# Row maxima of an attention turned into a row by fp32r products with a rounded identity

## The chip, the cores and the metric

The kernel runs on one core of a Trainium2 chip. The time is the device time of one execution of the program in microseconds. Three executions of the kernel before took 2443.36, 2448.75 and 2449.61 us; their median is 2448.75 us. The profile was taken from a further execution of its own, of 2449.5 us.

## What is computed

Two layers of a hybrid backbone work on 1024 latent tokens and 256 context tokens of width 1024. Each layer projects its input once, and the columns of the projection feed three groups of heads: a bidirectional RWKV-7 scan (6 heads), a grouped-query attention (6 query heads over 2 key heads) and a neighbourhood attention (4 heads). The part that matters here is the softmax of the two attentions:

```python
def one_block(qi):
    s = jnp.einsum('bqgrd,bsgd->bgrqs', qi, keys).astype(jnp.float32)
    p = jax.nn.softmax(s, axis=-1).astype(vals.dtype)
    return jnp.einsum('bgrqs,bsgd->bqgrd', p, vals)
...
s = jnp.concatenate([s_nb.reshape(B, H, GRID_W, n_nb), s_ctx], axis=-1)
p = jax.nn.softmax(s, axis=-1).astype(v.dtype)
```

Here `s_nb` holds the scores inside a query's grid window with a learned bias, and `s_ctx` its scores against all context keys. A softmax may subtract any number from all scores of a query before the exponential, as long as it is one number for the query; the kernel subtracts a rough row maximum.

## The kernel before

**Stages.** Each of the two layers runs an input projection (L203 to L205), then the scan of the RWKV heads, `rwkv` (L516 to L828), and beside it `attention` (L831 to L1133), then the output projection (L1196 to L1198). The program is written as one function after the other, but a scheduler orders each engine's instructions from a simulation of its own, so that the scan and the attention end up woven together on every engine. Each engine then takes its instructions strictly in that order, the DMA issues on SP included.

**The scan** is a chain of 40 steps in each layer: products with the state that wait for a DMA load of `X` (L706, L713), a copy (L716), products (L724), copies (L730), products (L734) and a decay on VectorE (L739). Between steps stand waves of preparation: a 16x16 inverse on VectorE (L653, L655) that goes out to DRAM through `inv_d` (L666) and comes back as `di` (L670).

**The attention** works on pairs of jobs. A job is 512 queries of one head (128 of the context), a pair is two such jobs, and there are 30 pairs in both layers together. `pair_max` finds the row maxima of one pair while `pair_main` does the exponentials and the products with the values of the pair before. In `pair_max`, for each tile of 128 queries:

- L894: rough scores `sm` = queries by keys, in up to three pieces of at most 512 keys, into PSUM;
- L896 or L898: VectorE reduces each piece to its maximum `mx`;
- L901: VectorE reduces the maxima of the pieces to one negated column of `nm`, a tile of 128 x 8 fp32 values, one column for each tile of queries;
- L907: once all columns stand, a TensorE product turns a column into a row: `nm`'s column is the stationary operand (128 x 1), the identity the moving one (128 x 128), and the row goes to partition 64 of `mt`;
- L908: ScalarE copies the row, rounded to fp32r, to partition 64 of the query tile `q[1]`.

`pair_main` then makes the scores `st` by two products, L963 with 128 rows and L964 with 65 rows, of which the last is this row of negated maxima against a row of ones in the keys. So L964 waits for L908, and L908 for L907. The exponential is L970 or L973, the sums are L977 or L982, the products with the values L948.

**Types.** The operands of L894, L963, L964 and of both projections are fp32r; those of L907, L948 and the scan are fp32. The profile has two records of TensorE for each fp32 product and one for each fp32r product. So the 180 products of L907 (two layers) are 360 records.

Of the kernel before, what the change touches and what calls it, by code (L numbers as in the profile page):

```python
# [8 lines left out]
F32 = mybir.dt.float32  # L9
F32R = mybir.dt.float32r  # L10
AF = mybir.ActivationFunctionType
ALU = mybir.AluOpType
AX = mybir.AxisListType
# [30 lines left out]
def body(tc, a):  # L44
    nc = tc.nc
# [4 lines left out]
    def cload(name, shape, eng):  # L50
        t = const.tile(shape, F32, tag="c_" + name, name="c_" + name)
        eng.dma_start(out=t, in_=a[name])
        return t

    silu = cload("c_col", [128, KT, 2], nc.sync)
    ident = cload("ident", [128, 128], nc.gpsimd)
# [25 lines left out]
    def mod_load(pool, l, g, k):  # L82
        wt = pool.tile([128, 1024], F32, tag="wm", name="wm")
        nc.sync.dma_start(out=wt, in_=a["wmod"][l, k, :, 1024 * g:1024 * g + 1024])
        return wt

    def mod_out(pt, l, g):
        mo = mods[l][:, 8 * g:8 * g + 8, :]
        nc.vector.tensor_tensor(out=mo, in0=pt, in1=bmod[:, l, 8 * g:8 * g + 8].unsqueeze(2).to_broadcast([128, 8, 2]), op=ALU.add)
        if g == 1:  # L90
            nc.vector.tensor_scalar(out=mo, in0=mo, scalar1=1.0, scalar2=None, op0=ALU.add)

    def mod_spread(groups, pool, psum):

        todo = [(l, g, k) for l, g in groups for k in range(KT)]
        acc = pool.tile([128, 256], F32, tag="am", name="am")
        silu32 = pool.tile([128, KT, 32], F32, tag="silu32", name="silu32")
        nc.gpsimd.memset(silu32, 0.0)
        nc.gpsimd.tensor_copy(silu32[:, :, 0:2], silu)
        nxt = mod_load(pool, *todo[0])  # L100
        yield
        for i, (l, g, k) in enumerate(todo):
            pm = psum.tile([128, 512], F32, tag="st", name="pmod")
            for j in range(4):
                nc.tensor.matmul(out=pm[32 * j:32 * j + 32, 0:256], lhsT=silu32[:, k, :], rhs=nxt[:, 256 * j:256 * j + 256],
                                 start=True, stop=True, tile_position=(0, 32 * j))
            if k == 0:
                nc.vector.tensor_copy(acc, pm[:, 0:256])
            else:
                nc.vector.tensor_tensor(out=acc, in0=acc, in1=pm[:, 0:256], op=ALU.add)  # L110
            if i + 1 < len(todo):
                nxt = mod_load(pool, *todo[i + 1])
            yield
            if k == KT - 1:
                pt = psum.tile([128, 512], F32, tag="st", name="pt")[:, 0:16].rearrange("p (m j) -> p m j", j=2)
                for m in range(8):
                    q, c = 32 * (m // 2), 128 * (m % 2)
                    nc.tensor.matmul(out=pt[:, m, :], lhsT=acc[:, c:c + 128], rhs=ident[:, q:q + 2], start=True, stop=True)
                mod_out(pt, l, g)
                yield  # L120
# [710 lines left out]
    def attention(l):  # L831
# [4 lines left out]
        ap1 = es.enter_context(tc.tile_pool(name=f"at{l}", bufs=1, **kw))  # L836
        ap2 = es.enter_context(tc.tile_pool(name=f"au{l}", bufs=2, **kw))
        pst = es.enter_context(tc.tile_pool(name=f"pst{l}", bufs=2, space=PSUM, side="right"))
        py = es.enter_context(tc.tile_pool(name=f"py{l}", bufs=1, space=PSUM, side="right"))
        wn = es.enter_context(tc.tile_pool(name=f"wn{l}", bufs=1, **kw))  # L840
        ms = mod_spread(((1, 2),) if last else ((0, 2), (1, 1), (1, 0)), wn, pst)
        onec = ap1.tile([128, 32], F32, tag="onec", name="onec")
        nc.vector.memset(onec, 1.0)

# [37 lines left out]

        def pair_max(q, k, jobs, nq, bias):

            nm = ap2.tile([128, 8], F32, tag="nm", name="nm")
            for i, job in enumerate(jobs):
                q0 = job["q0"]
                for qt in range(nq // 128):
                    qc = q0 + 128 * qt
                    pcs = job["parts"](qt)  # L890
                    mx = ap2.tile([128, 4], F32, tag="mx", name="mx", bufs=4)
                    for n_, (c0, o, bcol) in enumerate(pcs):
                        sp_ = pst.tile([128, 512], F32, tag="sm", name="sm", bufs=2)
                        nc.tensor.matmul(out=sp_[:, :o], lhsT=q[0][:, qc:qc + 128], rhs=k[0][:, c0:c0 + o], start=True, stop=True)  # L894
                        if bcol is None:
                            nc.vector.tensor_reduce(out=mx[:, n_:n_ + 1], in_=sp_[:, :o], op=ALU.max, axis=AX.X)  # L896
                        else:
                            nc.vector.tensor_tensor_reduce(out=sp_[:, :o], in0=sp_[:, :o], in1=bias[0][:, bcol:bcol + o], scale=1.0, scalar=-3.0e38,  # L898
                                                           op0=ALU.add, op1=ALU.max, accum_out=mx[:, n_:n_ + 1])
                        if n_ == len(pcs) - 1:  # L900
                            nc.vector.tensor_reduce(out=nm[:, 4 * i + qt:4 * i + qt + 1], in_=mx[:, :len(pcs)], op=ALU.max, axis=AX.X, negate=True)  # L901
                        yield
            for i, job in enumerate(jobs):
                q0 = job["q0"]
                mt = pst.tile([128, 512], F32, tag="sm", name="mt", bufs=2)
                for qt in range(nq // 128):
                    nc.tensor.matmul(out=mt[64:65, 128 * qt:128 * qt + 128], lhsT=nm[:, 4 * i + qt:4 * i + qt + 1], rhs=ident, start=True, stop=True, tile_position=(0, 64))  # L907
                nc.scalar.copy(q[1][64:65, q0:q0 + nq], mt[64:65, :nq])  # L908
                yield

# [189 lines left out]
        while True:  # L1100
            nxt = next(hs, None)
            mg = None
            npc = 0
            if nxt is not None:
                q, k, v, jobs, nq, och, bias = nxt
                mg = pair_max(q, k, jobs, nq, bias)
                npc = sum(len(j["parts"](t)) for j in jobs for t in range(nq // 128)) + 2
            if cur is not None:
                q, k, v, jobs, nq, och, bias = cur
                nit = len(jobs[0]["steps"]) + 1  # L1110
                done = 0
                old, tail[:] = tail[:], []
                for i, _ in enumerate(pair_main(*cur, nxt is None)):
                    for f in old[:1 if i + 2 < nit else None]:
                        f()
                        old.pop(0)
                    n_it += 1
                    if n_it >= 20 and n_it % 3 == 0:
                        next(ms, None)
                    while mg is not None and done < npc * (i + 1) // nit:  # L1120
                        next(mg, None)
                        done += 1
            if mg is not None:
                for _ in mg:
                    pass
            cur = nxt
            if cur is None:
                break
# [202 lines left out]
    for l in range(DEPTH):  # L1331
        lay = {}
        layer_proj(l, hd, fw, lay, lambda: rwkv(l, lay))
        attention(l)
        so = ExitStack()
        with ExitStack() as es:
            ow = out_weights(l, so, es)
        hd = None if l == DEPTH - 1 else open_h(l + 1)
        fw = out_proj(l, so, ow, a["xT"] if l == 0 else x2_d, x2_d if l == 0 else a["out"], hd)
# [89 lines left out]
```

## Time and profile before

| | us |
|---|---|
| median of three executions | 2448.75 |
| the profiled execution | 2449.5 |
| its span, from the first to the last instruction | 2447.7 |
| TensorE busy | 2206.0 (90%) |
| VectorE busy | 1615.7 (66%) |
| products of L907, 360 records, busy | 52.8 |
| attention of layer 0: first rough scores, last product with values | 570.7, 1194.3 |
| attention of layer 1: the same | 1803.5, 2316.8 |

A busy TensorE is not one at its peak: matmuls overlap at their ends, so the busy times of records overlap too, and the pace of a product is read from the starts of two that follow each other. Windows of the trace give the busy time of each engine in a stretch, and the granted clock of TensorE there as a share of full speed.

### The profile page before, as it was taken

To read this page: it belongs to the slowest core of one execution; us is meant where nothing else is said; L and a number is where in the kernel's file an instruction comes from. 1 tells how busy PE (TensorE), PEld (TensorE's weight loads), DVE (VectorE), ACT (ScalarE), POOL (GpSimd) and SP (SyncE) were. 2 spreads that over 40 slices of the span, in tenths; PEclk is the share of its full clock that TensorE was granted. 3 is DMA by queue.
4 is the path that set the end of the run, shared out by engine and by line. 5 is a ranking of instruction groups with operands and counts; after the bars stand their busy time and mean duration, and the time that the engine had idled before them with its cause. 6 is when DMAs were issued, how large, how long until landed. Compare 5 with 4: busy or idle time off the path is not lost. (4 is left out here: it accounts for less than half of the span.)

```text
span 2447.7 us, 57800 instructions
## 1 busy us (share of the span) xinstructions
PE 2206.0 (90%) x22616; PEld 1657.5 (68%) x22616; DVE 1615.7 (66%) x3063; ACT 1005.5 (41%) x2186; POOL 1180.5 (48%) x1438
## 2 busy tenths in 40 slices
PE   6999999997887898989999999899969888889897
PEld 3777898775555555555798777697746555556497
DVE  5687434445766878686387797524557788788746
ACT  3333413334544544454343443313345555545522
POOL 3465425424555555454155465533455565565453
PEclk9999999996887999989899999999968999999999
DMA  7344424527445544452233445335464545333342
GB/s 282 111 156 157 134 85 103 144 79 164 111 115 118 122 102 124 125 168 64 73 94 106 136 162 181 112 90 127 113 152 113 117 116 124 81 84 87 100 153 87
DMA packets 448241, 298.17 MB, mean 122 GB/s; under 512 B 249600, under 2 KB 395880, under 8 KB 446944
## 3 DMA queue, kind: packets, MB, share of 16 engines
q1 hardware_dynamic: 439936, 281.71, 41.9%
q0 software_dynamic: 7392, 10.28, 1.6%
q8 instruction: 178, 2.92, 0.5%
q10 hardware_dynamic: 640, 2.49, 0.4%
q14 instruction: 95, 0.78, 0.1%
HBM read 198.37 MB, written 91.79 MB: 119 GB/s over the span
## 5 line engine op out<-in xcount | busy, mean ns | idle before, releaser
L204 PE MATMUL pj<-hlo,wh 128*128 128x512 f32 (+1 forms) x1072 | 402.8, 376 | 13.1 <-DVE hlo L480 7.6
L203 PE MATMUL pj<-hhi,wh 128*128 128x512 f32 (+1 forms) x1072 | 403.2, 378 | 9.2 <-ACT qr L348 5.1
L205 PE MATMUL pj<-hhi,wl 128*128 128x512 f32 (+1 forms) x1072 | 402.0, 376 | 0.2 <-POOL wl L169 0.2
L204 PEld LDWEIGHTS pj<-hlo,wh 128*128 128x128 f32 x1072 | 205.7, 192 | 55.6 <-DVE hlo L480 7.7
L203 PEld LDWEIGHTS pj<-hhi,wh 128*128 128x128 f32 x1072 | 204.8, 192 | 54.3 <-issue 6.8
L169 POOL TENSOR_TENSOR wl<-wf,wh 128x512 fp32r<-128x512 f32 x104 | 142.9, 1379 | 202.7 <-ACT wh L168 185.4
L205 PEld LDWEIGHTS pj<-hhi,wl 128*128 128x128 f32 x1072 | 205.9, 192 | 38.6 <-issue 3.6
L896 DVE TENSOR_REDUCE mx<-sm 128x1 f32<-128x512 f32 (+1 forms) x372 | 199.1, 553 | 46.0 <-PE sm L894 43.7
L948 PE MATMUL y<-pt,v 128*64 128x256 f32 (+1 forms) x1392 | 214.0, 405 | 3.3 <-ACT pt L973 2.4
L970 ACT ACTIVATE pt<-st 128x512 f32<-128x512 f32 (+1 forms) x292 | 163.6, 583 | 129.5 <-PE st L964 125.7
L894 PE MATMUL sm<-k,q 128*128 128x256 f32 (+2 forms) x436 | 167.1, 429 | 34.6 <-DVE mx L896 26.8
L963 PE MATMUL st<-q,k 128*128 128x512 f32 (+3 forms) x376 | 165.9, 445 | 12.5 <-issue 3.5
L1197 PE MATMUL pj<-yl,wh 128*128 128x256 f32 x576 | 165.0, 289 | 2.0 <-POOL yl L1170 2.0
L1196 PE MATMUL pj<-yh,wh 128*128 128x256 f32 x576 | 162.8, 291 | 4.0 <-ACT wh L1147 2.1
L1198 PE MATMUL pj<-yh,wl 128*128 128x256 f32 x576 | 163.2, 288 | 0.1
L977 POOL TENSOR_TENSOR acc<-acc,pt 128x512 f32<-128x512 f32 x80 | 105.4, 1317 | 115.3 <-ACT pt L970 114.4
L948 PEld LDWEIGHTS y<-pt,v 128*64 128x64 f32 x1392 | 94.4, 144 | 90.8 <-issue 60.0
L894 PEld LDWEIGHTS sm<-k,q 128*128 128x128 f32 x436 | 82.8, 208 | 104.6 <-DVE mx L896 42.4
L964 PE MATMUL st<-q,k 65*128 65x512 f32 (+3 forms) x376 | 147.1, 395 | 0.6 <-ACT q L908 0.6
L625 DVE TENSOR_TENSOR G<-gt,msk 64x192 f32<-64x192 f32 (+1 forms) x320 | 110.5, 345 | 43.1 <-PE gt L620 32.0
L708 POOL MEMSET X<- 32x192 f32 x320 | 81.7, 255 | 89.1 <-PE py L754 59.9
L977 DVE TENSOR_TENSOR acc<-acc,pt 128x512 f32<-128x512 f32 x112 | 101.7, 918 | 30.3 <-ACT pt L970 29.8
(276 smaller groups left out, 5113.8 us busy)
## 6 DMA issues: line engine op xcount, KB each, us to landing
wf<-win SPq DMA_DIRECT2D x104, 256.0 KB
wm<-wmod SPq DMA_DIRECT2D x32, 512.0 KB
yf<-yg_d SPq DMA_DIRECT2D x72, 128.0 KB
wt<-wm SPq DMA_DIRECT2D x8, 1024.0 KB
gate_d<-o SPq DMA_DIRECT2D x32, 256.0 KB
wf<-wout SPq DMA_DIRECT2D x16, 512.0 KB
ldkk<-rw_d SPq DMA_DIRECT2D x40, 192.0 KB
ldkd<-rw_d SPq DMA_DIRECT2D x40, 192.0 KB
```

Source lines behind the costliest of these rows:

```text
L203: nc.tensor.matmul(out=ps[:, :n], lhsT=wh, rhs=hhi[:, k, t0:t0 + n], start=(k == 0), stop=False)
L204: nc.tensor.matmul(out=ps[:, :n], lhsT=wh, rhs=hlo[:, k, t0:t0 + n], start=False, stop=False)
L205: nc.tensor.matmul(out=ps[:, :n], lhsT=wl, rhs=hhi[:, k, t0:t0 + n], start=False, stop=(k == KT - 1))
L894: nc.tensor.matmul(out=sp_[:, :o], lhsT=q[0][:, qc:qc + 128], rhs=k[0][:, c0:c0 + o], start=True, stop=True)
L896: nc.vector.tensor_reduce(out=mx[:, n_:n_ + 1], in_=sp_[:, :o], op=ALU.max, axis=AX.X)
L948: mm = nc.tensor.matmul(out=y[64 * i:64 * i + 64, a0:a1], lhsT=v[:, t, :], rhs=pt[:, p0:p0 + a1 - a0], start=start, stop=stop and at == le ...
L963: nc.tensor.matmul(out=o, lhsT=k[0][:, 128 * t:128 * t + 128], rhs=q[0][:, qa:qb], start=True, stop=False)
L970: nc.scalar.activation(out=pt[:, :w], in_=sp_[:, :w], func=AF.Exp)
L977: eng.tensor_tensor(out=acc[i][:, :w], in0=sums[i][:, :w], in1=pt[:, :w], op=ALU.add)
L1196: nc.tensor.matmul(out=p_, lhsT=wh[m][:, k], rhs=yh, start=(x_ == 0), stop=False)
L1197: nc.tensor.matmul(out=p_, lhsT=wh[m][:, k], rhs=yl, start=False, stop=False)
L1198: nc.tensor.matmul(out=p_, lhsT=wl[m][:, k], rhs=yh, start=False, stop=(x_ == KT - 1))
```

## The change

The maxima are written to a tile `nm` of type fp32r, so that they are rounded as they are written, and turned into a row by one fp32r product with a copy of the identity that is rounded too. There are two such tiles, 128 x 72 each, made once per layer and used in turn. Columns 0 to 63 hold a part of the identity and are never written again; the maxima go to columns 64 to 71. The stationary operand of a product is a stretch of 65 columns that ends with the column of the maximum wanted, so that its row comes out in partition 64 of `mt`. Partitions 0 to 63 of `mt` are written too, and nothing reads them.

```diff
+        identr = ap1.tile([128, 128], F32R, tag="identr", name="identr")
+        nc.vector.tensor_copy(identr, ident)
+
+        nms = [ap1.tile([128, 72], F32R, tag=f"nm{i}", name="nm") for i in range(2)]
+        for z in nms:
+            nc.vector.tensor_copy(z[:, 0:64], ident[:, 0:64])
+            nc.vector.tensor_copy(z[:, 64:72], ident[:, 0:8])
+        nj = [0]
         onec = ap1.tile([128, 32], F32, tag="onec", name="onec")
...
-            nm = ap2.tile([128, 8], F32, tag="nm", name="nm")
+            nm = nms[nj[0] % 2]
+            nj[0] += 1
...
-                            nc.vector.tensor_reduce(out=nm[:, 4 * i + qt:4 * i + qt + 1], in_=mx[:, :len(pcs)], op=ALU.max, axis=AX.X, negate=True)
+                            nc.vector.tensor_reduce(out=nm[:, 64 + 4 * i + qt:65 + 4 * i + qt], in_=mx[:, :len(pcs)], op=ALU.max, axis=AX.X, negate=True)
...
-                    nc.tensor.matmul(out=mt[64:65, 128 * qt:128 * qt + 128], lhsT=nm[:, 4 * i + qt:4 * i + qt + 1], rhs=ident, start=True, stop=True, tile_position=(0, 64))
+                    nc.tensor.matmul(out=mt[0:65, 128 * qt:128 * qt + 128], lhsT=nm[:, 4 * i + qt:4 * i + qt + 65], rhs=identr, start=True, stop=True)
```

Lines behind the insertions stand 8 or 9 lower: L907 is L916 now, L894 is L903, L963 and L964 are L972 and L973, L948 is L957, L857 is L865.

The scheduler orders the instructions anew. Up to the first product of the row maxima in layer 0 TensorE's order is the same; from there it differs in many places, and so does that of the other engines. Two places are shown.

TensorE, layer 0, early in the attention (`mt` is the row of maxima, `ch` the chain of the scan, `st` the scores, `y` the product with the values, `gt` a preparation of the scan), before:

```order
L907 MATMUL mt<-c_ident,nm 1x128
L894 MATMUL sm<-k_10136,q_10142 128x256
L734 MATMUL ch<-X_2966,S_2954 64x64 x6
L734 MATMUL ch<-X_2966,S_2955 64x64 x6
L963 MATMUL st<-q_9991,k_9988 128x512
L964 MATMUL st<-q_9992,k_9978 128x512 x2
L907 MATMUL mt<-c_ident,nm 1x128 x2
L713 MATMUL ch<-X_2967,G_2952 32x64 x2
L713 MATMUL ch<-X_2967,G_2953 32x64 x2
```

The same place of the changed kernel:

```order
L916 MATMUL mt<-identr,nm 65x128
L903 MATMUL sm<-k_10142,q_10148 128x256
L972 MATMUL st<-q_9999,k_9996 128x512
L973 MATMUL st<-q_10000,k_9986 128x512
L734 MATMUL ch<-X_2966,S_2954 64x64 x6
L734 MATMUL ch<-X_2966,S_2955 64x64 x6
L973 MATMUL st<-q_10000,k_9986 128x512
L916 MATMUL mt<-identr,nm 65x128 x2
L972 MATMUL st<-q_9999,k_9996 128x512
L973 MATMUL st<-q_10000,k_9986 128x512
L957 MATMUL y<-pt_10168,v 64x256
L620 MATMUL gt<-G_2950,kb 64x128 x6
```

One pair of score products has moved ahead of the chain's L734, and the next step's L713, which followed the row maxima directly, now stands behind score products, products with the values and the `gt` of the scan.

SP, layer 0, an early wave of the scan beside the attention (`X` are the loads that L713 waits for, `inv_d` the inverse on its way out, `di` its way back, `stg` a load of keys), before:

```order
L706 DMA X_2967<-vt_d 32x3x64 x2
L666 DMA inv_d<-ee 12x32x16
L761 DMA y_d<-yst 32x4x192 x4
L666 DMA inv_d<-ee 12x32x16 x7
L706 DMA X_2967<-vt_d 32x3x64 x2
L670 DMA di<-inv_d 128x768
L857 DMA stg<-k_d 64x1280 x2
```

The same place of the changed kernel:

```order
L666 DMA inv_d<-ee 12x32x16 x4
L761 DMA y_d<-yst 32x4x192 x4
L666 DMA inv_d<-ee 12x32x16 x4
L706 DMA X_2967<-vt_d 32x3x64 x2
L670 DMA di<-inv_d 128x768
L706 DMA X_2967<-vt_d 32x3x64 x2
L865 DMA stg<-k_d 64x1280 x2
```

The first two of the four loads of a step's `X` have moved behind the writes of `inv_d`, and the last two behind the load of `di`, which waits until those writes have landed. `X` loads directly behind the `di` load stand in two waves beside layer 0's attention before and in four with the change, and in none and two beside layer 1's.

On VectorE the five copies to `identr` and the two `nm` tiles stand ahead of the memset of `onec`, which was the first of the attention's instructions there; the wait in front of it is the same.

## The prediction

> **What bounds the kernel now.** I read the page first, for the busy share of each engine and its course over the span, then windows over the attention of both layers, then the waits of TensorE in them, and last the chain of work that ended last.
>
> ```profile
> span 2447.7 us, 57800 instructions
> PE 2206.0 (90%) x22616; PEld 1657.5 (68%) x22616; DVE 1615.7 (66%) x3063; ACT 1005.5 (41%) x2186; POOL 1180.5 (48%) x1438
> PE   6999999997887898989999999899969888889897
> ```
>
> TensorE is the busiest engine, and its digits fall to 7 and 8 only where the scan and the attention run side by side. Windows give, for each engine, busy time and records, then TensorE's granted clock, the DMA share and GB/s:
>
> ```profile
> 570.00:1000.00 430.00, 366.98 (x5671) 244.32 (x5668) 317.10 (x846) 205.99 (x523) 223.92 (x319) 0.85 0.50 117
> 1000.00:1200.00 200.00, 186.03 (x1599) 110.53 (x1600) 135.63 (x253) 97.74 (x205) 85.06 (x76) 0.91 0.34 100
> 1800.00:2320.00 520.00, 457.78 (x6840) 294.03 (x6836) 417.18 (x1007) 262.78 (x624) 282.16 (x368) 0.94 0.43 102
> ```
>
> The first window is layer 0's attention beside the scan: TensorE idles 63 of 430 us. The second is mostly what of that attention is left: it idles 14 of 200. The third is layer 1's, where it idles 62 of 520 and VectorE is busy for 80%. What TensorE waits for there, layer 0 first (total us, times, longest):
>
> ```profile
> PE sm L894 <- DVE mx L896: 13.5, 12, 2.4
> PE py L754 <- DVE tt L689: 8.7, 5, 3.4
> PE ch L713 <- DMA X<-vt_d: 8.7, 4, 4.4
> ...
> PE sm L894 <- DVE mx L896: 13.4, 11, 3.4
> PE ch L713 <- POOL X L708: 8.1, 4, 3.0
> ```
>
> No wait is large. TensorE's queue, with short waits on the scan's other engines, sets the pace; in the second window it is nearly alone.
>
> **The change part by part.** First the pace of a product. The group of the old one (busy, mean ns, idle before it), then starts in the timeline: one batch of old records and what follows it; fp32r products of 128 columns that follow each other; one whose neighbour's weights were loaded early; and fp32r products of 256 columns.
>
> ```profile
> L907 PE MATMUL mt<-c_ident,nm 128*1 128x128 f32 x360 | 52.8, 291 | 2.5 <-DVE mx L896 1.7 <-DVE nm L901 0.5 <-DVE mx L898 0.3
> ...
> 2010.67 1.69 PE L907 MATMUL mt<-c_ident,nm 128*1 128x128 f32 x14
> 2012.29 0.49 PE L577 MATMUL pcu<-tri,th 128*128 128x128 f32 x2
> ...
> 768.61 0.28 PE L964 MATMUL st<-q,k 65*128 65x128 f32 x1
> 768.72 0.27 PE L963 MATMUL st<-q,k 128*128 128x128 f32 x1
> 768.83 0.28 PE L964 MATMUL st<-q,k 65*128 65x128 f32 x1
> ...
> 915.97 0.22 PE L964 MATMUL st<-q,k 65*128 65x128 f32 x1
> 916.03 0.45 PE L894 MATMUL sm<-k,q 128*128 128x512 f32 x1
> ...
> 1289.86 0.28 PE L1198 MATMUL pj<-yh,wl 128*128 128x256 f32 x1
> 1289.98 0.28 PE L1196 MATMUL pj<-yh,wh 128*128 128x256 f32 x1
> ```
>
> *Old:* 14 records hold the queue from 2010.67 to 2012.29, so 0.116 us each and, with two records to a product, 0.23 us. *New:* no row shows 65 stationary by 128 moving columns. Fp32r products of 128 by 128 columns follow each other by 0.11 us; the one at 915.97 lets the next start after 0.06; those of 256 moving columns keep 0.12 with as many stationary ones, so at 128 moving columns the load of the weights looks like the limit. Hence 0.06 to 0.11; I take 0.07, near the low row, because the new load is half as wide. It could cost less than that only by costing less than the 128 columns that it streams, so nothing lies below. A product saves 0.16 of 0.23 us, **70%**, and 180 of them 29 us of TensorE's queue.
>
> [...]
>
> Next, how much of it lies on the path. Records and busy time of L907 in the three windows (TensorE, then the weight loads), and its longest pieces in the chain of work that ended last, which this view follows back only into layer 1 (start, us):
>
> ```profile
> 570.00:1000.00 430.00, 18.16 (x124) 9.15 (x124) 0.85 0.50 117
> 1000.00:1200.00 200.00, 12.64 (x76) 6.31 (x76) 0.91 0.34 100
> 1800.00:2320.00 520.00, 22.03 (x160) 12.66 (x160) 0.94 0.43 102
> ...
> 1838.19 3.50 PE mt L907 x16
> 2010.74 1.62 PE mt L907 x14
> 2199.44 1.62 PE mt L907 x14
> 2247.84 1.62 PE mt L907 x14
> 2291.59 1.92 PE mt L907 x16
> 2293.53 0.45 ACT q L908
> ```
>
> The five pieces are 10.3 us, 47% of layer 1's 22.03. I give layer 0's first window the same share, 8.5 of 18.16, and its second window, where TensorE hardly idles, all of 12.64.
>
> - *Layer 0's rest of attention:* 70% of 12.64 is **8.8 us**, and I count it whole: what is next late there is TensorE's own next product.
> - *Beside the scan:* 70% of 8.5 + 10.3 is 13.1 us at most and nothing at least, since a scan step that is freed earlier may wait for VectorE or POOL (the waits above). Neither end is nearer; I take half, **6.6 us**.
> - *The path through one pair* (L907, L908, then the scores) gets shorter too; the last piece above, at 2291.59, is a pure case of it, and it is in the sum already.
>
> The added copies on VectorE are bounded by these rows:
>
> ```profile
> L492 DVE CAST aw<-s 96x384 fp32r<-96x384 f32 x4 | 2.8, 708 | 0.2 <-DMA s<-a 0.2
> L1189 DVE MEMSET ones<- 128x128 f32 x2 | 0.3, 165 | 0.0
> ```
>
> One of 128 columns takes 0.165 to 0.71 us, those of 64 and 8 at most that; five a layer are below 2.7 us in both layers, and I take **1.0 us** in all, near the row of the same width. They stand ahead of the attention while the scan runs; I charge them in full, since the scan's own VectorE work is behind them. Writing the column of maxima as fp32r I cost at nothing: the reduction reads what it read. Nor does the wider output cost anything: a product streams its 128 columns whatever stands beside them, and ScalarE reads partition 64 as before. No wait is new: each product waited for its reduction before, and the copies for what the memset of `onec` waited for.
>
> What the new order moves I cannot sum from rows; I look at it as a rival. Sum: 2449.5 - 8.8 - 6.6 + 1.0 = **2435.1 us**, against the profiled execution, which lies 0.75 above the median of the runs.
>
> **The rivals.**
>
> *Nearly all of it counts.* For it: TensorE is busy for 85 to 93% of the windows. Against: the waits above stay. With all of the 13.1 us it is 2428.6, with the whole 29 us of the queue 2421.5.
>
> *The load of the weights is exposed*, 0.11 us a product: the gain is 15.4 x 52 / 70 = 11.4, less the copies: 2439. For it stand the 0.11 us pairs at 768.61; against it, that their load is twice as wide. [...]
>
> *The scan keeps its pace.* Its chain through VectorE, DMA and POOL sets the steps, and what TensorE saves turns into idle time; 8.8 us remain of layer 0's rest, of which two late loads of `X` at 3.1 us (next) take 6.2 and the copies 1.0: 2448.
>
> *Slower: the loads of X.* In the new order of SP, in four more waves than before, loads of `X` stand directly behind the load of `di`, which waits until the writes of the inverse have landed. How far apart these are on SP now:
>
> ```profile
> 1833.99 3.65 SPq L666 DMA_DIRECT2D inv_d<-ee  x8
> 1840.73 0.33 SPq L670 DMA_DIRECT2D di<-inv_d  x1
> ```
>
> From the last issue of `inv_d` (1837.64) to `di` are 3.1 us, with other issues between, and the longest wait of L713 for such a load is 4.4. If each of the four is fully late and TensorE only waits there, the scan gains nothing: 2449.5 - 8.8 + 1.0 + 4 x 4.4 = **2459**. It decides once the loads land after the decay (L739) of the step before. Against it: loads run ahead of the chain by up to two of three buffers, and only four waits for `X` are in the list of layer 0 now. The same stretch of TensorE's order, with score products moved ahead of L734 and L713, fits either: they fill a wait for `X`, or cause one.
>
> *The product is no faster* (0.23 us as now): 2450.5. The rows of L964 leave little room for it.
>
> **How the numbers follow.** Chances: forecast 0.40 (2430 to 2441), nearly all 0.15, exposed load 0.10, scan keeps its pace 0.17, slower 0.15, no faster product 0.03. The predicted time is 2435. About 0.3% is what a measurement of this kernel can tell from no change: 2441.4 and 2456.1 around the median. Faster takes nearly all of the first three, less the part of the exposed load and of the forecast that ends above 2441: 0.60. Slower has most of its own rival: 0.15. The same holds the rest, 0.25. The range reaches from 2421, all of the queue's relief, to 2459, the late loads.
>
> **What would show it.** Right: 180 records of the new product in place of 360, batches of eight that hold the queue for about 0.6 us, the last rows before 2318 us closer together, and layer 0's attention ending some 12 us earlier. Wrong: records of 0.11 us pace (exposed load); L713 waiting for `X` longer than 8.7 us in layer 0 (late loads); the scan's steps as long as before with more idle time of TensorE (the scan keeps its pace). The forecast falls if the scan's last step comes later than now, for then the order and not the product decides.

## The result, and the profile after

The changed kernel takes **2434.33 us** (median of 11 executions, 2424.62 to 2441.11) beside 2448.75 us for the kernel before on the same chip (11 executions, 2440.74 to 2453.78). The ratio is **0.9942**, 95% interval 0.9924 to 0.996. The profiled execution took 2430.72 us, with a span of 2428.9. The forecast was 2435 us and faster; number and sign came out right. The experiments show that much of the way there was not the one that the prediction took.

The page of the changed kernel, the same three rows as before:

```profile
span 2428.9 us, 57402 instructions
PE 2184.2 (90%) x22436; PEld 1645.6 (68%) x22436; DVE 1616.8 (67%) x3073; ACT 1008.5 (42%) x2186; POOL 1187.6 (49%) x1438
PE   6999999996979888989999999999878888889797
```

TensorE has 180 records fewer and is busy 21.8 us less, the span is 18.8 us shorter, and its share of the span is the same 90%. The pace of the new product, from its group and two places of TensorE's timeline (start, length of the piece):

```profile
L916 PE MATMUL mt<-identr,nm 128*65 128x128 f32 x180 | 25.0, 252 | 4.6 <-DVE mx L905 3.6 <-DVE nm L910 0.5 <-DVE mx L907 0.5
...
1975.49 0.40 PE L916 MATMUL mt<-identr,nm 128*65 128x128 f32 x4
1975.73 0.51 PE L635 MATMUL kt<-c_ident,kb 128*128 128x128 f32 x3
...
761.21 0.70 PE L916 MATMUL mt<-identr,nm 128*65 128x128 f32 x8
761.84 0.65 PE L957 MATMUL y<-pt,v 128*64 128x128 f32 x6
```

Four products hold the queue for 1975.73 - 1975.49 = 0.24 us, **0.060 us** each; the batch of eight takes 0.63, which is 0.079 each. Over the whole trace, from one such product to a next one at full clock, the median is 0.062 us and the middle half lies between 0.059 and 0.080; between two records of the old product it is 0.109. The windows of both layers (length, busy time and records of each engine, granted clock, DMA share, GB/s) and the first waits of TensorE in layer 0, as they were read before:

```profile
570.00:1000.00 430.00, 370.89 (x5814) 248.52 (x5815) 331.67 (x881) 216.73 (x546) 232.61 (x328) 0.86 0.51 121
1000.00:1200.00 200.00, 188.67 (x1556) 123.31 (x1555) 130.57 (x228) 93.06 (x193) 88.60 (x78) 0.91 0.38 109
1800.00:2320.00 520.00, 454.02 (x6452) 293.69 (x6453) 399.78 (x945) 262.29 (x618) 281.82 (x357) 0.91 0.43 106
...
PE py L754 <- DVE tt L689: 14.8, 6, 4.8
PE sm L903 <- DVE mx L905: 12.6, 13, 2.3
PE ch L713 <- DMA X<-vt_d: 7.2, 3, 4.9
```

Two things are to be seen. The first window holds 143 more records of TensorE than before (5814, for 5671), although each product of the maxima has one record less: work has moved forward. And the clock granted in layer 1 is 0.91, where it was 0.94; over that attention's own stretch of the changed kernel, 1768.6 to 2291.4 us, it is 0.90.

### The profile page after: what moved, and what is told of

Read it like the earlier page. It is cut to its first block, busy times and chain, and to the rows that moved or that the text cites. A ratio compares the mean times of both kernels' runs of the same rounds, so it can differ in the third digit from the quotient of the medians.

```text
span 2428.9 us, 57402 instructions
## 1 busy us (share of the span) xinstructions
PE 2184.2 (90%) x22436; PEld 1645.6 (68%) x22436; DVE 1616.8 (67%) x3073; ACT 1008.5 (42%) x2186; POOL 1187.6 (49%) x1438
## 5 line engine op out<-in xcount | busy, mean ns | idle before, releaser
L957 PE MATMUL y<-pt,v 128*64 128x256 f32 (+1 forms) x1392 | 217.2, 406 | 0.9 <-ACT pt L982 0.9
L903 PE MATMUL sm<-k,q 128*128 128x256 f32 (+2 forms) x436 | 168.2, 425 | 28.6 <-DVE mx L905 21.3
L972 PE MATMUL st<-q,k 128*128 128x512 f32 (+3 forms) x376 | 170.8, 458 | 12.0 <-ACT pt L979 3.5
L1205 PE MATMUL pj<-yh,wh 128*128 128x256 f32 x576 | 162.7, 290 | 11.8 <-ACT yh L1178 8.2
L957 PEld LDWEIGHTS y<-pt,v 128*64 128x64 f32 x1392 | 95.7, 146 | 92.8 <-issue 64.2
L973 PE MATMUL st<-q,k 65*128 65x512 f32 (+3 forms) x376 | 151.6, 406 | 5.0 <-ACT q L917 4.9
L903 PEld LDWEIGHTS sm<-k,q 128*128 128x128 f32 x436 | 84.1, 206 | 91.9 <-DVE mx L905 34.5
## 6 DMA issues: line engine op xcount, KB each, us to landing
yf<-yg_d SPq DMA_DIRECT2D x72, 128.0 KB
```

What stands on the lines that cost most here:

```text
L957: mm = nc.tensor.matmul(out=y[64 * i:64 * i + 64, a0:a1], lhsT=v[:, t, :], rhs=pt[:, p0:p0 + a1 - a0], start=start, stop=stop and at == le ...
L972: nc.tensor.matmul(out=o, lhsT=k[0][:, 128 * t:128 * t + 128], rhs=q[0][:, qa:qb], start=True, stop=False)
L973: mm = nc.tensor.matmul(out=o, lhsT=k[1][0:65, 128 * t:128 * t + 128], rhs=q[1][0:65, qa:qb], start=False, stop=True)
L1205: nc.tensor.matmul(out=p_, lhsT=wh[m][:, k], rhs=yh, start=(x_ == 0), stop=False)
```

## The experiments

The change does two things: it shortens a product, and it makes the scheduler order everything anew. To have the one without the other, each engine's instructions were held in an order written out beforehand, by edges between neighbours that are marked as without a semaphore (`NoSync`):

```diff
         body(tc, aps)
+        _pin(nc, tc, _EXTRA)
...
+    info = mybir.DependencyInfo(mybir.DependencyClass.NoSync, mybir.DependencyReason.DATA)
...
+        for a, b in zip(seq, seq[1:]):
+            tc.add_manual_dep(b, a.name, info, reason="order")
```

The table has all runs. Product and order (layer 0 / layer 1) say what was taken from the kernel before ("old") and from the changed one ("new"). The ratio is to the kernel before on the same chip. The rest is from the one profiled execution of each: granted clock, TensorE's busy time, the length of layer 0's attention (first rough scores to last product with values), the part of it behind the last L713 of layer 0's scan, and layer 1 from its first rough scores to the end of the span; all in us, from the starts of these lines in the traces.

| run | product | order | ratio, 95% interval | clock | TensorE busy | layer 0's attention | its rest | layer 1 to end |
|---|---|---|---|---|---|---|---|---|
| before | old | old/old | 1 | 0.934 | 2206.0 | 623.6 | 140.9 | 644.2 |
| e4 | old | old/old | (one execution) | 0.933 | 2199.2 | 623.6 | 142.0 | 646.6 |
| e1 | new | old/old | 0.9973, 0.9952 to 0.9995 | 0.927 | 2182.2 | 625.0 | 144.8 | 638.6 |
| e9 | new | old/old | 0.9979, 0.9957 to 1.0001 | 0.930 | 2181.6 | 612.1 | 136.8 | 644.7 |
| e7 | new, twice | old/old | 0.9993, 0.9975 to 1.0011 | 0.932 | 2193.2 | 614.5 | 143.4 | 651.7 |
| e11 | new | old/new | 1.0019, 0.9993 to 1.0045 | 0.923 | 2194.4 | 621.7 | 141.3 | 657.9 |
| e6 | old | new/old | 0.9964, 0.9942 to 0.9986 | 0.937 | 2194.5 | 613.9 | 128.0 | 648.8 |
| e2 | old | new/new | 1.0019, 0.999 to 1.0048 | 0.937 | 2200.8 | 612.7 | 127.8 | 660.6 |
| e12 | old | new/new | 1.0004, 0.9979 to 1.0029 | 0.939 | 2193.0 | 607.7 | 127.5 | 654.6 |
| after | new | new/new | 0.9942, 0.9924 to 0.996 | 0.926 | 2184.2 | 598.7 | 126.6 | 660.3 |
| e8 | new | new/new | 0.9915, 0.9884 to 0.9945 | 0.930 | 2181.9 | 604.4 | 125.8 | 652.7 |
| e5 | new | new, SP's end old | 0.9945, 0.992 to 0.9969 | 0.930 | 2180.0 | 593.4 | 125.6 | 658.6 |
| e3 | new | new/old | 0.9898, 0.9878 to 0.9918 | 0.928 | 2187.6 | 604.7 | 128.1 | 643.8 |
| e10 | new | new/old | 0.9909, 0.9875 to 0.9942 | 0.924 | 2188.6 | 606.2 | 127.1 | 650.9 |

The runs' orders differ in nothing else but these: e5 is told below; the five copies of the changed kernel stand where they stand in it whenever the product is new.

### The product and the order apart: e1, e2, e3, e4

> The changed products (fp32r, 65 by 128), with every engine's instructions held in the order of the kernel before; only the five copies a layer are added. If the gain is the price of the product (theory), this is 9 to 16 us faster than before, with both layers' attention shorter. If it is the new order that gained (rival), it stays within 4 us of before. If both are needed, it lies between: 4 to 9 us faster.

> The products of before (fp32, 1 by 128), with every engine's instructions held in the order of the changed kernel, without the copies. Theory (price of the product): within 4 us of before, or up to 6 us slower, since the order was made for a shorter product. Rival (order): 9 to 16 us faster than before.

> The changed products, with the new order in layer 0 and the order of before in layer 1. In the two profiles layer 0's attention ends 25 us earlier, and layer 1's attention and the end take 16 us longer with the change. If the new order of layer 1 costs that, this is 5 to 12 us faster than the changed kernel (about 2426). If the 16 us are scatter between executions or come from the product, it is within 4 us of the changed kernel.

> The kernel before once more, for a second profile of it: how far the end of layer 0's attention (1194.3 us) and the length of layer 1's (513 us) scatter between two executions of one program. Theory and rivals differ by 10 to 25 us in these stages; if the scatter is under 5 us the stages of single profiles can be compared.

Measured: 2434.68 us (e1), 2443.48 (e2) and 2418.31 (e3), beside 2440.36 for the kernel before on this chip; e4, the kernel before once more, 2448.02. Neither half alone brings what the change brings: the product alone 0.27%, the order alone nothing that can be told from zero, both 0.58%. The order of the changed kernel in layer 0 with that of before in layer 1 (e3; the cut lies between the layers, where both orders have issued the same instructions) is the fastest, at 0.9898; beside the changed kernel's 0.9942 that is some 11 us, inside the 5 to 12 expected.

The rest of layer 0's attention, by windows from the scan's last L713 to the last product with values, in the order before, e1, e9, e2, after:

```profile
1053.40:1194.30 140.90, 130.79 (x852) 76.86 (x843) 91.55 (x163) 67.08 (x135) 56.11 (x44) 0.88 0.33 98
...
1052.90:1197.70 144.80, 132.54 (x825) 79.83 (x814) 91.09 (x160) 66.43 (x134) 56.32 (x44) 0.83 0.31 94
...
1043.00:1179.80 136.80, 124.98 (x820) 74.78 (x813) 90.45 (x162) 66.90 (x135) 58.07 (x44) 0.89 0.33 100
...
1055.80:1183.60 127.80, 119.75 (x788) 69.64 (x777) 89.36 (x148) 63.96 (x126) 57.67 (x43) 0.91 0.34 104
...
1042.40:1169.00 126.60, 118.36 (x767) 70.23 (x755) 89.53 (x148) 63.99 (x126) 58.02 (x43) 0.88 0.35 105
```

What shortens this stretch is the order, which leaves fewer records in it (788 for 852 with the same old product). The new product in the old order leaves it at 136.8 to 144.8 us, on both sides of the old product's 140.9 and 142.0. In e1 the stretch has 27 records fewer than before, and yet TensorE is busy longer, 132.54 for 130.79 us: its clock is 0.83 for 0.88.

### The SP queue at the end, the product's worth in the better order, the product twice: e5 to e8

The new order's layer 1 is slower, and its end looked like a matter of SP's queue: seven loads of `yf` stand ahead of the last two stores of `gtl` before the change, and one with it. e5 puts 26 issues of SP back. e6 is e3 with the old product. e7 is e1 with each product issued a second time:

```diff
                     nc.tensor.matmul(out=mt[0:65, 128 * qt:128 * qt + 128], lhsT=nm[:, 4 * i + qt:4 * i + qt + 65], rhs=identr, start=True, stop=True)
+                    nc.tensor.matmul(out= mt[0:65, 128 * qt:128 * qt + 128], lhsT=nm[:, 4 * i + qt:4 * i + qt + 65], rhs=identr, start=True, stop=True)
```

> The changed kernel in its own order, but for 26 issues of SP behind layer 1's attention, which stand as before the change: seven loads of yf ahead of the last two stores of gtl, not one. If those stores, which wait for VectorE's gtl, held the loads behind them back: from layer 1's last product of py to the end about 130.5 us, for 137.5 in the changed kernel (before the change 131.0 and 130.4), layer 1's attention unchanged at about 523, and the time about 7 us below the changed kernel's, near 2427. Rival: the end is longer because the attention's own last pieces come in another order on TensorE and VectorE; then it stays at 137 to 138 and the time at 2434.

> The old product in the order of the third run (of the change in layer 0, of before in layer 1): with that run (2418.31 us) it gives the product's worth in the better order. Granted clocks so far: 0.933 to 0.937 with the old product, 0.926 to 0.928 with the new one. If the shorter product leaves TensorE's 3.4 us windows emptier, and the clock halves in more of them: clock 0.933 or more here, layer 0's attention 610 to 614 (604.7 with the new product), layer 1's 513 to 517, the end 130, time about 2428: 10 us above, where the queue is 29 us longer. Rival, the product's saving counts nearly whole: 2440 or more. Rival, it is worth nothing and the order is everything: within 3 us of 2418.

> The changed product in the order of before (as the first run, 2434.68 us), but each product issued twice into the same place: 180 more records of 0.06 us, 10.8 us more of TensorE's queue. If the queue's length counts: 5 to 11 us later than the first run, 2440 to 2446, and layer 0's attention 628 to 631 for its 625.0. If what is saved on the queue is lost to the clock: fewer half-speed windows than the first run, clock 0.929 to 0.934 for its 0.927, and the time within 3 us of it.

> The changed kernel once more, beside the other runs on one chip: 2434 us by its own comparison; how far its stages scatter from one execution to another. Layer 0's attention 598.7, layer 1's 522.8, the end 137.5, clock 0.926, each within 3 us and 0.003 if they are the order's and the product's own.

Measured, beside 2442.14 us for the kernel before: e5 2430.06, e6 2435.25, e7 2443.69, e8 2423.88.

**e5 refutes my reading of SP's queue.** From the last product with values to the end are 2425.5 - 2285.2 = 140.3 us, not 130.5. SP's timeline there shows why, with the last rows of the scan's products `pso` (L799) behind it:

```profile
2279.30 9.65 SPq L806 DMA_DIRECT2D yg_d<-yo  x2
2290.67 0.91 SPq L1153 DMA_DIRECT2D wf<-wout  x2
2291.62 3.47 SPq L1175 DMA_DIRECT2D yf<-yg_d  x7
2296.59 0.33 SPq L1153 DMA_DIRECT2D wf<-wout  x1
2296.97 1.09 SPq L1042 DMA_DIRECT2D yg_d<-gtl  x2
...
L799 PE MATMUL pso<-c_ident,yo x12: 272/273/328, 2252.6 to 2284.3; 128*128 128x128 f32 x12
```

The seven loads now stand ahead of the stores, but all of them stand behind the store of `yo` (L806), the scan's own last output, on which SP waits until 2288.95. That store waits for the last L799, at 2284.3, which the new order puts 25 places later on TensorE, among the last products with values. In e3, with the old order there, the last L799 starts at 2280.0 and the first output product at 2292.9; in e5 at 2284.3 and 2297.0: 12.9 and 12.7 us apart, and between 12.6 and 14.1 in all fourteen profiles, while from the last product with values to the first output product are 5.9 to 6.6 us in the old order and 11.8 to 13.2 in the new one. So in the new order layer 1's output projection hangs on this last product of the scan. TensorE's timeline in e5 has no gap ahead of L799, and one of 6.37 us ahead of the output projection:

```profile
2282.61 1.51 PE L957 MATMUL y<-pt,v 128*64 128x256 f32 x10
2284.05 0.55 PE L799 MATMUL pso<-c_ident,yo 128*128 128x128 f32 x3
2284.53 1.08 PE L957 MATMUL y<-pt,v 128*64 128x256 f32 x6
...
2296.95 0.80 PE L1205 MATMUL pj<-yh,wh 128*128 128x256 f32 x2 [6.37 <-ACT yh L1178]
```

It is L799's place in TensorE's order, then, and not a late scan, that holds the projection back. In e3 the projection starts without a gap behind the attention's own last products, so there both ends meet. That L799 was not moved alone.

**e6** came out between its theories. Against e3 the product is worth 0.9964 - 0.9898 = 0.66% in this order, some 16 us, more than the 10 of the one theory and less than the 20 and more of its rival. The clock, layer 0's attention and the end are as expected (0.937, 613.9, 130.2); layer 1's attention, 518.6, lies just above its 513 to 517. **e7** lies between its theories. Its 2443.69 us can't be held against e1's 2434.68, which comes from another chip; by the ratios it is 3 to 5 us later than e1 and e9 (0.9993 beside 0.9973 and 0.9979), where the longer queue asked for 5 to 11 and the clock for at most 3. Layer 1 is longer, as with a longer queue; layer 0's attention, 614.5, is not the 628 to 631 of that theory; the clock, 0.932 in the profile and 0.930 in the mean of its ten executions, is the other theory's 0.929 to 0.934. **e8** missed three of its four bounds: layer 0's attention is 604.4 for 598.7, layer 1's 513.5 for 522.8, the clock 0.930 for 0.926; its time by its own comparison is 0.9915, for 0.9942, with intervals that overlap. Single executions scatter by 6 to 9 us in a stage here, and by 13 in layer 0 between e1 and e9 (that the kernel before has 623.6 twice was chance), so only what all profiles of a kind have in common can be read from them.

### Once more, for what is common: e9 to e12

> The first run once more (changed product, order of before), to know its worth and its stages better: 0.9973 then, layer 0's attention 625.0 us, the rest of it behind the scan's last step 144.7 at a granted clock of 0.83, mean clock 0.927, while the product issued twice gave 614.5 and 143.3. If the shorter product alone gains next to nothing in layer 0 because the clock is halved in more windows: ratio 0.996 to 0.999, layer 0's attention 615 to 626, clock 0.926 to 0.930. If the first run's profile was an odd one, and the queue's 29 us count: ratio 0.992 or less, layer 0's attention below 610.

> The third run once more (changed product; the changed order in layer 0 and that of before in layer 1), the fastest so far at 0.9898 by its own comparison, 0.9942 and 0.9915 for the changed kernel. If layer 1's new order costs 8 to 16 us from its first row maxima to the end (652.7 to 660.6 in the four profiles with it, 638.6 to 651.6 in the six with the old one): 0.987 to 0.992, and that stretch 640 to 648 us. If the difference is scatter of single executions: 0.992 to 0.995.

> Changed product; the order of before in layer 0 and the changed order in layer 1: the other half. If the layers' orders act apart: layer 0's attention as in the first run, 615 to 625 us, from layer 1's first row maxima to the end 652 to 661, so some 12 us slower than the first run: ratio 1.000 to 1.004. If layer 1's cost is only the shift that layer 0's earlier end brings to it: 640 to 648 there, and a ratio of 0.995 to 0.998.

> The second run once more (old product, changed order): 1.0019 then, layer 0's attention 612.7 us, from layer 1's first row maxima to the end 660.6, clock 0.937. If the new order gains some 11 us in layer 0 and loses 8 to 16 in layer 1: 0.999 to 1.004, with the clock at 0.933 or more. If the order alone brings what the changed kernel gained: 0.992 to 0.995.

Measured, beside 2441.04 us: e9 2432.49, e10 2416.09, e11 2446.24, e12 2440.37. The order that is new in layer 0 alone is again the fastest (0.9909); it lies below the changed kernel in both comparisons, though the intervals overlap. The ratios fall where the theories of separate layers put them (e10 to e12) and that of the clock (e9); of the stages e9's layer 0 (612.1, for 615 to 626) and e10's layer 1 (650.9, for 640 to 648) lie just outside. What all profiles have in common:

- **Layer 0's attention.** Old product and old order 623.6 twice; new product, old order 612.1 to 625.0; old product, new order 607.7 to 613.9; both new 593.4 to 606.2.
- **Layer 1 to the end.** Old order 638.6 to 651.7 (eight profiles, mean 646.2), new order 652.7 to 660.6 (six, mean 657.5), whatever the product: the new order costs **11 us** there. The ratios say the same: from e1 and e9 to e11 0.43%, from e6 to e2 and e12 0.48%, 10 to 12 us.
- **Clock.** Old product 0.933 to 0.939 (five profiles), new product 0.923 to 0.930 (eight), new product twice 0.932. Over all executions see below.

TensorE's waits of layer 1 that come with the new order, in the kernel before first, then in the changed kernel, e11 and e12:

```profile
PE mg L684 <- DVE di L687: 1.1, 2, 0.8
PE pj L1196 <- ACT yh L1169: 0.7, 1, 0.7
...
PE pj L1205 <- ACT yh L1178: 8.2, 1, 8.2
PE mg L684 <- DVE di L687: 6.3, 2, 6.1
...
PE pj L1205 <- ACT yh L1178: 6.9, 1, 6.9
PE mg L684 <- DVE di L687: 6.7, 2, 6.6
...
PE mg L684 <- DVE di L687: 7.6, 2, 7.5
PE pj L1196 <- ACT yh L1169: 7.0, 1, 7.0
```

The wait of `pj` is the output projection of e5; the other a round trip of the scan's inverse at the attention's start, where the order leaves TensorE nothing else. Part of it is an exchange: before, a wait for VectorE's maxima stood at that place. Neither was undone alone, so that these two make up the 11 us is read, not shown.

## Why the clock matters here

The five profiles with the old product have TensorE busy for 2193.0 to 2206.0 us, 2198.7 in the mean, the eight with the new one for 2185.1: 13.6 us less. The queue got shorter by 180 x (0.23 - 0.06) = 30.6 us. So the other work became some 17 us longer.

The trace can tell whether the clock did that, since it gives the granted clock of every window: in the traces before and after it is 1.00 or 0.50, over stretches that are multiples of 3.41 us. Busy time in a window of half speed is counted half, and the rest in full; that is TensorE's work at full clock. It is 2065.2 to 2074.8 us in the five profiles (mean 2070.8) and 2035.1 to 2043.1 in the eight (2039.4): 31.4 us less, all that the queue saved. What half speed adds to it is 118.9 to 138.1 us in the five (127.9) and 137.9 to 157.4 in the eight (145.7): **17.7 us** more. So on the average of these profiles the clock takes back more than half of the saving, and that is the 17 us. With the order held, it is 8.5 us (old/old), 26.0 (new/old) and 18.1 (new/new), from one to three profiles each. That half speed is real shows in one product: records of L907 in the kernel before follow each other by 0.109 us at full clock and by 0.213 in such windows (medians).

That the shorter product lowers the clock doesn't rest on single profiles. The granted clock is on record for each execution of these runs, and here are the means with the order held and the product alone changed: old/old 0.935 with the old product (80 executions) and 0.927 with the new one (24); new/old 0.937 (10) and 0.929 (12); new/new 0.936 (22) and 0.929 (27, e5 among them). Single executions overlap, from 0.926 to 0.944 and from 0.918 to 0.939. The product issued twice, in the old order, has 0.930 (10): with a part of the length back, a part of the clock is back.

Where it goes shows in windows of 3.41 us. The kernel before first, then e1 at the same place of the same order:

```profile
1109.18:1112.60 3.42, 1.49 (x8) 0.64 (x7) 3.42 (x3) 1.69 (x3) 3.34 (x2) 0.99 0.76 231
1112.60:1116.01 3.41, 2.70 (x10) 1.49 (x11) 2.10 (x6) 0.00 (x0) 3.22 (x3) 0.50 0.00 2
1116.01:1119.42 3.41, 3.41 (x19) 2.14 (x21) 0.17 (x1) 1.96 (x4) 0.96 (x2) 0.51 0.00 0
1119.42:1122.84 3.42, 3.42 (x29) 2.28 (x29) 1.52 (x7) 2.17 (x7) 0.49 (x1) 1.00 0.33 91
```

```profile
1112.29:1115.71 3.42, 1.48 (x8) 0.63 (x7) 3.42 (x3) 1.67 (x3) 3.34 (x2) 1.00 0.67 224
1115.71:1119.12 3.41, 2.31 (x10) 1.53 (x10) 2.05 (x6) 0.80 (x2) 3.18 (x3) 0.50 0.00 0
1119.12:1122.53 3.41, 3.18 (x17) 2.15 (x17) 1.43 (x5) 1.53 (x4) 1.45 (x2) 0.50 0.00 0
1122.53:1125.95 3.42, 3.42 (x16) 2.67 (x16) 0.41 (x2) 2.48 (x8) 0.21 (x1) 0.50 0.45 134
1125.95:1129.36 3.41, 3.41 (x16) 2.76 (x16) 1.18 (x2) 0.23 (x2) 1.21 (x2) 0.50 0.25 77
1129.36:1132.77 3.41, 3.41 (x40) 3.11 (x40) 1.70 (x4) 0.98 (x4) 1.87 (x3) 1.00 0.09 21
```

TensorE is busy for 1.49 and 1.48 us of the first window and idles for the rest of its 3.42, waiting for VectorE (busy throughout; in the kernel before the wait for the maxima of L896 is 2.24 us), and the next one is granted 0.50 of the clock. Before, TensorE is busy for 2.70 us of it and all of the one after, and full speed returns after two windows. In e1 it has less to do there, 2.31 and 3.18 us, and half speed lasts for four windows, of 10 to 17 records each. The window that starts at 1122.53 is busy throughout and yet followed by another at half speed, while before the one at 1116.01 was the last. Nor does a fall always stand behind idle time: in the kernel before, TensorE is busy for all 3.40 us from 907.80 to 911.20, at a clock of 1.00, and the next 3.40 us are granted 0.50. How the shorter product leads to more half-speed windows is read from this place alone, and chance has its part in it. In e9 the same idle stretch falls across two windows, in which TensorE is busy for 2.76 and 2.72 us of 3.40, and the clock stays at 1.00:

```profile
1100.80:1104.20 3.40, 2.76 (x16) 1.34 (x12) 2.96 (x8) 2.09 (x4) 3.32 (x2) 1.00 0.57 206
1104.20:1107.60 3.40, 2.72 (x24) 1.99 (x24) 1.79 (x5) 2.39 (x7) 3.32 (x4) 1.00 0.00 0
1107.60:1111.00 3.40, 3.19 (x22) 2.28 (x21) 2.27 (x4) 1.46 (x5) 2.05 (x3) 1.00 0.36 103
```

## Why the prediction came out, step by step

- **The pace of the product** (0.07 us, bounds 0.06 to 0.11): right: 0.060 in the batch of four, 0.062 in the median, 0.079 in the batch of eight. The rival of the exposed load, 0.11 us and so 52% of 0.23 saved, falls with it. That the load of the weights sets the 0.11 us of products of 128 by 128 columns was the author's estimate. That a product takes its moving columns' time whatever stands beside them holds between fp32 records of 128 moving columns: ten with 128 stationary ones (L319) hold the queue of the kernel before from 134.24 to 135.33 us, 0.109 us each, and records of L907, with one, are 0.109 us apart in the median.
- **29 us of TensorE's queue**: right as a length at full clock (30.6 by the pace, 31.4 by TensorE's work at full clock), wrong as time. The prediction took every other duration as fixed; TensorE's busy time fell by 13.6 us, since half speed added 17.7.
- **Layer 0's rest of attention, 8.8 us counted whole**: this step failed. "What is next late there is TensorE's own next product" is not what the runs show. In the old order the new product leaves the rest at 144.8, 136.8 and 141.3 us (e1, e9, e11), 141.0 in the mean, for 141.4; in the new order at 125.6 to 128.1, 126.6 in the mean, for 127.8. That is 0.4 and 1.1 us, where 28 and 19 products at 0.17 us would save 4.8 and 3.2; the first of these is within the scatter of three profiles. The 14 us that this stretch lost in the changed kernel are the order's, which moved work ahead of the scan's last step. The count itself was too large as well: of the 76 records in the prediction's window only 56 stand behind the scan's last step.
- **Beside the scan, half of 13.1 us**: layer 0's part of it, half of 70% of 8.5, is 3.0 us. Layer 0's attention up to the scan's last L713 shrank from 482.2 us (before and e4) to 478.7 (e1, e9, e11) in the old order, and from 483.7 (e2, e6, e12) to 474.8 (after, e8, e5, e3, e10) in the new one: 3.5 and 8.9 us. Profiles of one kind differ by up to 11 us there, so that the term depends on the order is read, not shown. In layer 1 the product moved nothing that rises above the scatter.
- **The copies, 1.0 us**: they take 3.0 us of VectorE in both layers together, more than the 2.7 that were to bound them, since one 128x128 copy alone took 1.33. Layer 0's first rough scores start at 570.3 us, for 570.7 before, so nothing of it shows on the path. The groups:

```profile
L843 DVE CAST identr<-c_ident 128x128 fp32r<-128x128 f32 x2 | 1.5, 770 | 0.0
L847 DVE CAST nm<-c_ident 128x64 fp32r<-128x64 f32 x4 | 0.9, 240 | 0.0
L848 DVE CAST nm<-c_ident 128x8 fp32r<-128x8 f32 x4 | 0.6, 153 | 0.0
```

- **The new order, left out of the sum**: its total is near zero with the old product (ratios 1.0019 and 1.0004), but it is made of -12 us in layer 0's attention (623.6 to a mean of 611.4) and +11 from layer 1's first scores to the end. With the new product its layer 0 is worth 0.72% (0.9976, the mean of e1 and e9, to 0.9904, that of e3 and e10), twice the 0.36% of e6.
- **The rival of the late `X` loads** didn't come: TensorE's waits for them in layer 0 are 7.2 us, for 8.7. At the load of `di` SP waited for the writes of `inv_d` 16 times before and 17 times with the change, 0.6 and 0.7 us at most. Its sign was right for layer 1, its mechanism was not.
- **The rival of the scan that keeps its pace** was nearer than the forecast for the product in the old order: 0.9976 (the mean of e1 and e9) of 2441 is a gain of 6 us, the rival gave the 1.5 us between 2449.5 and 2448, the forecast 14.4. In the new orders the product is worth more: 0.60% from e6 to e3 and e10, 0.83% from e2 and e12 to the changed kernel and e8, some 15 and 20 us. Why an order lets more of it count was not tested.

So the number held by compensation, which is luck: the product alone gained 6 us and not 14.4, layer 0's order and the product together 23 (0.9904), and layer 1's order gave back some 3 to 9 of these by the ratios (0.9942 and 0.9915), 11 by the traces. In the two profiles layer 0's attention ended 25.3 us earlier (1169.0, for 1194.3), twice the 12 that were to show the forecast right, and layer 1 from its first scores took 16.1 us longer. What stays open is why the old order keeps only 6 us, when the clock takes back some 18 of 31 in the mean.

## What to carry to other kernels

Where a scheduler orders the program, a cheaper instruction is two changes; price them apart, and by layer, since the new order can win in one and lose in the other. Before counting a shorter queue as time, look at the granted clock: here its mean was 0.928 with the shorter product, for 0.935, and half speed took back 17.7 of the 31.4 us saved. And ask what each stage's end hangs on: here layer 0's hung on the attention, layer 1's on one late product of the scan, and the same order was good for the one and bad for the other.

## What was not expected of the hardware

An fp32r product of 65 stationary and 128 moving columns takes 0.060 us in a batch of four, for the 0.23 us of an fp32 one with a single stationary column and the same moving ones. The granted clock fell to 0.50, in steps of 3.41 us, after the two windows above in which TensorE was busy for less than half (1.48 and 1.49 of 3.42 us). Its mean over the span is lower with less work for TensorE: 0.928 in 73 executions with the new product, for 0.935 in 112 with the old one, and half speed takes back 17.7 of the 31.4 us that were saved.
